# Other places in the tile for the split weights, sums taken earlier, and activations split ahead of weights, in a decoder layer

## The chip, the core and the metric

The kernel runs on one core of a Trainium2 chip. The metric is the device time of one execution in microseconds (us), the median of three runs. A separate execution was taken by the hardware profiler; everything that is said of single instructions comes from it. The engines are called as the profile calls them: PE does the matrix products (PEld is its loading of the stationary operand), DVE and ACT are the vector and the scalar engine, POOL a general engine, and SP issues most DMAs.

## The reference

One decoder layer in float32 on 256 tokens of width 2048, cut here to what the change touches:

```python
h = rms_norm(x, mix_pre_norm)
y = hybrid_mixer(h, w_in, ..., w_branch_a, w_branch_b, w_mix_out)      # mLSTM and RWKV-7 side by side
x = x + rms_norm(y, mix_post_norm)
h = rms_norm(x, xattn_pre_norm); m = rms_norm(mem, mem_norm)
x = x + rms_norm(cross_attention(h, m, xattn_wq, xattn_wkv, xattn_wo), xattn_post_norm)
h = rms_norm(x, ffn_pre_norm)
u = h @ ffn_w_up                                                      # 2048 -> 16384
uc = conv_b + sum(conv_w[j] * shift_right(u, 2 - j) for j in range(3))
x = x + rms_norm((gelu(gate) * up) @ ffn_w_down, ffn_post_norm)       # gate, up = halves of uc
```

Nearly all of the arithmetic is in the products with the large weight matrices: `w_in`, the two branch matrices, `w_mix_out`, the four of the cross-attention, `ffn_w_up` and `ffn_w_down`.

## The kernel before

**How a product is made.** Every float32 operand of a large product is split into a high and a low part in the type float32r: high is a rounded copy (ACT), low is the rest (DVE). A product is then three products on PE: high by high, high by low, low by high. In the code `wh` and `wl` are the parts of a chunk of weights, `xh` and `xl` those of the activations.

**Blocks and chunks.** The program is a list of blocks, each 512 (or 1024) output columns wide. The weights of a block come in chunks of 512 KB: 128 partitions by 1024 floats. `run()` (L433) goes through the chunks of all blocks in one order that `visits()` lays down, 648 chunks with an index `i`. In a block of kind "fm" a chunk holds two slices (`kj`) of 512 columns; the weights are PE's stationary operand, 128 by 128 at a time, and the activations, 128 by 256, the moving one. That makes 2 slices x 4 column groups x 3 products, 24 products a chunk. The fm blocks are those of `w_in` (except four), `w_br`, `w_mo`, `w_xk`, `w_xq`, `w_xo` and `w_fu`. In a block of kind "tm" the activations are stationary and the weights move: 512 columns in four blocks of `w_in` and in `w_fd`, 296 in the small block `w_sm`, and 256 at a time in `w_xv`. The up-projection `w_fu` has the 256 chunks from i = 264, `w_fd` the 128 behind them.

**The feed.** `Feed` (L338) keeps PE supplied. `dma` loads a chunk into one of four `raw` buffers, `hi` casts it to `wh` on ACT (L376), `lo` subtracts to `wl` on DVE (L397), each a few chunks ahead of the products. `staged` (L357) gives the place of a chunk's parts in their tile: the tiles are 1152 floats long, and the 1024 floats start at an offset `o` in floats. Before, `o` is 0 for tm, and for fm it is 16, except that every fourth chunk (i divisible by 4; in the up-projection by 16) starts at 24. `wh` and `wl` have four buffers each, and the offset is the same in both.

**Side work.** Everything else (the mLSTM and RWKV recurrences, the softmax, norms, convolution) is cut into pieces by generators and put between the products by `side.half()`, which is called at each chunk and between its two slices. The engines' queues run in the order in which this program is written. The side work has small products of its own on PE: transposes (vt, haT, yT, xt), products of the recurrences (gram, lv, X, U, Tn, Y, num, den, zg), and the sums of the norms (st, stb).

**The places that the change touches.** `Stat.last` (L271) makes the norm after the last cross-attention block: it folds the sum of squares so far, squares the last two column groups on ACT, sums all over partitions by three products with ones (stb; each is two instructions on PE), and takes Ln and Exp on ACT. Until that is done the up-projection's first products can't start. The last `w_xo` block is "bankwise": all its products for the first two column groups come first, then those of the third, then those of the fourth, which goes to a bank of its own (`apart`), so that the squares can begin early. In `run()` the chunks that a block holds back for such an order are the `tail`: two here, four at the end of `w_fd`. For a tail the weights' parts are made first (`feed.lo`), and then the activations' parts are asked for (`b["xs"]`), which for `w_fd` splits them at that moment (`asplit`). In the program's first block the three products of a column group follow each other, wl last.

Of the kernel before, what the change touches and what calls it, by code (L numbers as in the profile page):

```python
# [11 lines left out]
AF = mybir.ActivationFunctionType  # L12
# [133 lines left out]
def _layer(ctx, tc, nc, d, dbg):  # L146
# [21 lines left out]
    def C(name, tag, shape=None, dt=F32):  # L168
        return mp.tile(shape or [P, S], dt, tag=tag, bufs=1, name=name)
# [73 lines left out]
    class Stat:  # L243
# [24 lines left out]
        def fold(self):  # L268
            dve.tensor_add(self.acc[:, 0], self.acc[:, 0], self.acc[:, 1])

        def last(self, src, tag, meanwhile):  # L271

            self.fold()
            sq = C("sql", tag, [P, 2, S])
            for j in range(2):
                act.activation(sq[:, j], src[j], AF.Square)
            q = aux("stb", [P, S])
            for i, v in enumerate((self.acc[:, 0], sq[:, 0], sq[:, 1])):
                mm(q, ones.broadcast_to((P, P)), v, start=(i == 0), stop=(i == 2))
            meanwhile()  # L280
            self.rb = cp.tile([P, S], F32, tag="strb", bufs=1, name=self.name + "_b")
            act.activation(self.rb, q, AF.Ln, scale=1.0 / D, bias=epsc)
            act.activation(self.rb, self.rb, AF.Exp, scale=-0.5)
            self.done = True

# [38 lines left out]
    def block(kind, srcs, xs, evac, before=None, cols=512, pool_=None, pre=None, bankwise=False, tail=0):  # L324
# [2 lines left out]
                           pool=pool_ or acc, pre=pre, task=None, bankwise=bankwise, tail=tail))  # L327
        return blocks[-1]

    class Feed:  # L330
        def __init__(self, order):
            self.kind = [k for k, s in order]
# [38 lines left out]
        def hi(self, upto):  # L371
# [60 lines left out]

    def run():  # L433
        order = visits()
        feed = Feed([(b["kind"], s) for b, c0, c1 in order for s in b["srcs"][c0:c1]])
        feed.begin()
        for c in range(1, 8):
            x_load(c)
# [3 lines left out]
        for b, c0, c1 in order:  # L442
# [23 lines left out]
            for ci, s in enumerate(srcs):  # L466
                if b["pre"]:
                    b["pre"](ci, feed)
                feed.lo(i + 1)
                side.half()  # L470
                side.more = lambda: feed.hi(i + 2)
                ahead = b["xs"](k)
                feed.lo(i + 3)
                feed.dma(i + 6)
                wh, wl = feed.st.pop(i)
                for kj in range(s.shape[1]):
                    xh, xl = b["xs"](k) if kj else ahead
                    first, last = k == 0, k == nk - 1
                    if b["kind"] == "fm":
                        steps = []  # L480
                        for m in range(nm):
                            o = banks[m // 2][:, m % 2]
                            a, c = wh[:, kj, m * P:(m + 1) * P], wl[:, kj, m * P:(m + 1) * P]
                            steps.append([(o, a, xh, first and m % 2 == 0, False), (o, c, xh, False, last),
                                          (o, a, xl, False, False)])
                        if first and entry and b is entry[0]:
                            steps = [[v[0] for v in steps], [v[1] for v in steps], [v[2] for v in steps]]
                        else:
                            steps = [[v[0], v[2], v[1]] for v in steps]
# [860 lines left out]
    def y_evac(b, st, key, gname):  # L1350

        def gen(ps):
# [1 line left out]
                M[key] = [U("z0"), U("z1")]  # L1354
            z = M[key][b // 2]

            last = [ps[1][:, 0], xo3["apart"]] if b == 3 and key == "z2" else []

            def carry(g, js=(0, 1)):
                for j in js:  # L1360
                    m = (b % 2) * 4 + g * 2 + j
                    act.activation(z[:, m], last[j] if g and last else ps[g][:, j], AF.Copy, scale=pcol(gname, b * 4 + g * 2 + j))

            if last:
                st.add(ps[0])
                carry(0)
                st.last(last, "bg0", lambda: carry(1, (0,)))
                yield
                carry(1, (1,))
                yield  # L1370
                return
            for g in range(2):
                st.add(ps[g])
                carry(g)
# [1 line left out]
            if b == 3:  # L1376
                yield from st.column_of_sums()
        return gen

    def part(v, k2):  # L1380
        return v[k2 // 4][:, (k2 % 4) * 2:(k2 % 4) * 2 + 2]
# [276 lines left out]
        side.need(side.add(xo()))  # L1658

    for b in range(4):  # L1660
        xo3 = block("fm", W("w_xo", b), lambda k: (M["oT"][:, 0, k], M["oT"][:, 1, k]), y_evac(b, st3, "z2", "xpostg"),
              before=need_o if b == 0 else None, bankwise=b == 3)


    stf = Stat("stf")
# [289 lines left out]
```

## Time and profile before

| | |
|---|---|
| median of three runs | 1885.58 us (1885.05 to 1885.87) |
| the profiled execution | 1884.58 us |
| its span in the trace | 1882.5 us |
| granted clock of PE | 0.999 |
| fm products (128x256), all kinds | 11,328, mean duration 277 to 281 ns |
| tm products of 512 columns with `as` | 1,536, mean duration 389 to 390 ns |
| ACT casts to `wh` (L376) | 640, mean 1043 ns |
| DVE subtractions to `wl` (L397) | 640, mean 1217 ns |

Times in the trace count from the start of the span. Products on PE overlap: one lasts some 280 ns in the profile, but the next starts some 115 ns after it. So a product's cost is read from start to start, or as the length of a stretch through its count. The duration of a matmul is modelled at its end, and moves with that distance only in part. In a row of the timeline the first number is the start and the second the duration, both in us; what stands in brackets is the idle time ahead of the instruction and what ended it.

### The profile page before, as it was taken

Reading aid. Unit: us, or ns where it says so; the run is one execution under the profiler, and the core shown is the slowest. Engines: PE = TensorE matmul, PEld = TensorE weight load, DVE = VectorE, ACT = ScalarE, POOL = GpSimd, SP = SyncE. Lnnn points to the kernel's source line nnn. Section 1 sums busy time; section 2 is a strip of 40 time slices with the busy share of each in tenths; the row PEclk is TensorE's granted clock in tenths of the full one; section 3 lists DMA queues with packets and bytes.
Section 4 is the critical chain, followed back from the end, with each engine's and each line's share of the span. In section 5 each row is a group of like instructions: output and inputs, shape, how many; then the busy total and the mean of one; then the engine's idle time right before and its main releaser. Section 6 shows DMA issues by size and latency. Waiting matters only on the chain.

```text
span 1882.5 us, 36361 instructions
## 1 busy us (share of the span) xinstructions
PE 1872.3 (99%) x15024; PEld 1783.9 (95%) x15024; DVE 1293.9 (69%) x1832; ACT 1016.4 (54%) x1477; POOL 21.3 (1%) x40
## 2 busy tenths in 40 slices
PE   9999999999999999999999999999999999999998
PEld 9999988999999999999999999999999988888886
DVE  7788787566675857677766666677666675556555
ACT  6776445555454645666554445554454555445544
POOL 0000000000000000000000000000000000000000
PEclk9999999999999999999999999999999999999999
DMA  7545544344556765455666666666666666666664
GB/s 260 187 163 198 179 146 161 131 147 157 169 174 209 265 204 182 138 193 180 190 190 192 197 194 192 193 189 192 196 196 193 195 191 214 194 193 194 192 192 142
DMA packets 98197, 351.46 MB, mean 187 GB/s; under 512 B 11056, under 2 KB 11568, under 8 KB 97648
## 3 DMA queue, kind: packets, MB, share of 16 engines
q1 hardware_dynamic: 97168, 348.01, 57.8%
q8 instruction: 117, 1.92, 0.4%
q10 hardware_dynamic: 864, 1.15, 0.2%
q14 instruction: 48, 0.39, 0.1%
HBM read 347.01 MB, written 2.10 MB: 185 GB/s over the span
## 4 chain that ended last, share of the span: by engine, by line
PE 97%; DVE 1%; ACT 1%; DMA 0%; issue 0%; ACTq 0%; DVEq 0%
PE fm L181 68%; PE tm L181 25%; DVE wl L397 1%; PE gram L181 0%; PE Y L181 0%; PE lv L181 0%; PE num L181 0%; ACT wh L376 0%; DMA w<-in_w_in_dram 0%; DVE rows L66 0%; PE X L181 0%; PE gramA L181 0%; PE U L181 0%; PE zg L181 0%; PE zwa L181 0%
## 5 line engine op out<-in xcount | busy, mean ns | idle before, releaser
L397 DVE TENSOR_TENSOR wl<-raw,wh 128x1024 fp32r<-128x1024 f32 (+1 forms) x640 | 776.2, 1217 | 428.9 <-ACT wh L376 424.5
L376 ACT CAST wh<-raw 128x1024 fp32r<-128x1024 f32 (+1 forms) x640 | 664.8, 1043 | 512.8 <-PE fm L181 387.2
L181 PE MATMUL fm<-fh,wh 128*128 128x256 f32 x2048 | 567.3, 277 | 1.4 <-ACT fh L66 1.4
L181 PE MATMUL fm<-fh,wl 128*128 128x256 f32 x2048 | 566.5, 277 | 0.0
L181 PE MATMUL fm<-fl,wh 128*128 128x256 f32 x2048 | 566.3, 277 | 0.0
L181 PEld LDWEIGHTS fm<-fh,wh 128*128 128x128 f32 x2048 | 384.9, 188 | 1.5 <-ACT fh L66 1.5
L181 PEld LDWEIGHTS fm<-fh,wl 128*128 128x128 f32 x2048 | 384.9, 188 | 0.2 <-DVE wl L397 0.2
L181 PEld LDWEIGHTS fm<-fl,wh 128*128 128x128 f32 x2048 | 384.9, 188 | 0.0
L181 PE MATMUL tm<-wh,as 128*128 128x512 f32 x1024 | 315.8, 390 | 0.8 <-DVE as L66 0.8
L181 PE MATMUL fm<-hh,wh 128*128 128x256 f32 x1024 | 287.7, 281 | 0.0
L181 PE MATMUL fm<-hh,wl 128*128 128x256 f32 x1024 | 285.7, 279 | 1.2 <-DVE wl L397 1.0
L181 PE MATMUL fm<-hl,wh 128*128 128x256 f32 x1024 | 285.3, 279 | 0.0
L181 PEld LDWEIGHTS tm<-wh,as 128*128 128x128 f32 x1024 | 192.2, 188 | 40.9 <-DVE as L66 1.1
L181 PE MATMUL tm<-wl,as 128*128 128x512 f32 x512 | 199.3, 389 | 0.0
L181 PEld LDWEIGHTS fm<-hh,wl 128*128 128x128 f32 x1024 | 193.0, 188 | 2.1 <-DVE wl L397 1.4
L181 PEld LDWEIGHTS fm<-hh,wh 128*128 128x128 f32 x1024 | 193.4, 189 | 1.3
L181 PEld LDWEIGHTS fm<-hl,wh 128*128 128x128 f32 x1024 | 193.1, 189 | 0.1
L181 PEld LDWEIGHTS tm<-wl,as 128*128 128x128 f32 x512 | 96.1, 188 | 20.0
L66 ACT CAST as<-ac 128x256 fp32r<-128x256 f32 x128 | 45.6, 404 | 110.8 <-PE tm L181 110.8
L66 DVE TENSOR_TENSOR as<-ac,as 128x256 fp32r<-128x256 f32 x128 | 48.6, 421 | 61.7 <-ACT as L66 61.7
L181 PE MATMUL fm<-mgh,wh 128*128 128x256 f32 x256 | 71.4, 279 | 0.0
L181 PE MATMUL fm<-mgl,wh 128*128 128x256 f32 x256 | 71.2, 278 | 0.0
(383 smaller groups left out, 2223.9 us busy)
## 6 DMA issues: line engine op xcount, KB each, us to landing
raw<-in_w_fu_dram SPq DMA_DIRECT2D x256, 512.0 KB, 4.2
raw<-in_w_in_dram SPq DMA_DIRECT2D x152, 512.0 KB, 3.5
raw<-in_w_fd_dram SPq DMA_DIRECT2D x128, 512.0 KB, 3.9
raw<-in_w_br_dram SPq DMA_DIRECT2D x32, 512.0 KB, 3.8
raw<-in_w_mo_dram SPq DMA_DIRECT2D x32, 512.0 KB, 4.2
raw<-in_w_xk_dram SPq DMA_DIRECT2D x8, 512.0 KB, 3.6
raw<-in_w_xv_dram SPq DMA_DIRECT2D x8, 512.0 KB, 3.6
raw<-in_w_xq_dram SPq DMA_DIRECT2D x8, 512.0 KB, 3.8
```

Source lines behind the costliest of these rows:

```text
L66: return f(out, *a, **k)
L181: pe.matmul(out, lhsT, rhs, start=start, stop=stop, skip_group_check=True)
L376: nc.scalar.copy(wh, r)
L397: nc.vector.tensor_sub(wl, r, self.st[self.nl][0])
```

## The change

It has five parts.

1. The places. For fm chunks `o` is now 24 throughout. For tm it stays 0 where 512 columns move, and becomes 8 for the small block and for `w_xv`, which gets a kind of its own in the feed. A table `KICK` names 22 chunks, all of kind fm, that have one half at another place: with 0 the first slice lies at 16 and the second at 24, with 1 the first at 24 and the second at 48 (16 beyond a multiple of 32). They stand at the begin of a stretch behind side products, or in the middle of a chunk where these come between its slices. The regular change of place every four or sixteen chunks is gone.
2. The first block. For the first two chunks the products go by groups of four: all high by high, then activations low, then weights low.
3. The tails. The activations' parts are asked for ahead of the weights' parts.
4. The last `w_xo` block. The squares and the sum of its first two column groups, and the fold, come directly after those groups and ahead of the next weights. Ahead of the last six products the square of the third group is taken, and the products with ones for the fold and for this square are made. Only the fourth group's square and product come after the last product.
5. `Stat.last` keeps Ln and Exp; the products with ones are in `ones_of`.

```diff
-        def last(self, src, tag, meanwhile):
-
-            self.fold()
-            sq = C("sql", tag, [P, 2, S])
-            for j in range(2):
-                act.activation(sq[:, j], src[j], AF.Square)
-            q = aux("stb", [P, S])
-            for i, v in enumerate((self.acc[:, 0], sq[:, 0], sq[:, 1])):
-                mm(q, ones.broadcast_to((P, P)), v, start=(i == 0), stop=(i == 2))
-            meanwhile()
+        def ones_of(self, vs, start=False, stop=False):
+            if start:
+                self.q = aux("stb", [P, S])
+            for i, v in enumerate(vs):
+                mm(self.q, ones.broadcast_to((P, P)), v, start=start and i == 0, stop=stop and i + 1 == len(vs))
+
+        def last(self):
...
+    KICK = {16: 0, 26: 1, 32: 0, 52: 1, 60: 0, 104: 0, 108: 0, 111: 0, 116: 0, 117: 1, 120: 1, 134: 0, 140: 0, 144: 1,
+            159: 1, 168: 0, 215: 0, 218: 1, 235: 0, 242: 0, 256: 0, 280: 1}
...
             k, c = r.shape[1:]
-            up = i - len(self.src) + 384
-            o = 0
-            if self.kind[i] == "fm":
-                o = 16 if i % (16 if up >= 0 else 4) else 24
+            kick = KICK.get(i)
+            e = -(-c // 64) * 64
+            o = 24 if self.kind[i] == "fm" else 0 if c >= 512 and self.kind[i] == "tm" else 8
+            if kick is not None:
+                o, e = (16, e + 8) if kick == 0 else (o, e + 24)
             w = wp.tile([P, 1024 + 128], F32R, tag=name, bufs=4, name=name)
-            e = -(-c // 64) * 64
             return w[:, o:o + k * e].rearrange("p (k c) -> p k c", k=k)[:, :, 0:c]
...
-        feed = Feed([(b["kind"], s) for b, c0, c1 in order for s in b["srcs"][c0:c1]])
+        feed = Feed([("xv" if b is xv else b["kind"], s) for b, c0, c1 in order for s in b["srcs"][c0:c1]])
...
+                        elif b is blocks[0] and k < 4:
+                            steps = [[v[0] for v in steps], [v[2] for v in steps], [v[1] for v in steps]]
...
             if nt:
 
+                ahead = [b["xs"](k + j) for j in range(sum(s.shape[1] for s in tail))]
                 feed.lo(i + nt - 1)
...
-                        steps.append((w[0][:, kj], w[1][:, kj]) + tuple(b["xs"](k)))
+                        steps.append((w[0][:, kj], w[1][:, kj]) + tuple(ahead[len(steps)]))
...
+                            if g and ti == 2 * n - 2:
+                                b["mid"](banks)
...
                     if g == 0:
+                        if b["bankwise"]:
+                            b["after"](banks)
                         feed.lo(i + 1)
...
+    def y_last(b, st, key, gname):
+        def carry(src, m):
+            act.activation(M[key][b // 2][:, (b % 2) * 4 + m], src, AF.Copy, scale=pcol(gname, b * 4 + m))
+
+        def after(ps):
+            st.add(ps[0])
+            st.fold()
+
+        def mid(ps):
+            M["sql"] = C("sql", "bg0", [P, 2, S])
+            act.activation(M["sql"][:, 0], ps[1][:, 0], AF.Square)
+            for j in range(2):
+                carry(ps[0][:, j], j)
+            st.ones_of((st.acc[:, 0], M["sql"][:, 0]), start=True)
+
+        def gen(ps):
+            end = xo3["apart"]
+            act.activation(M["sql"][:, 1], end, AF.Square)
+            st.ones_of((M["sql"][:, 1],), stop=True)
+            carry(ps[1][:, 0], 2)
+            st.last()
+            yield
+            carry(end, 3)
+            yield
+        return after, mid, gen
```

More of the change, by code (lines that the diff above doesn't have):

```diff
@@ L269, in fold @@
             dve.tensor_add(self.acc[:, 0], self.acc[:, 0], self.acc[:, 1])
-        def last(self, src, tag, meanwhile):
-            self.fold()
-            sq = C("sql", tag, [P, 2, S])
-            for j in range(2):
-                act.activation(sq[:, j], src[j], AF.Square)
-            q = aux("stb", [P, S])
-            for i, v in enumerate((self.acc[:, 0], sq[:, 0], sq[:, 1])):
-                mm(q, ones.broadcast_to((P, P)), v, start=(i == 0), stop=(i == 2))
-            meanwhile()
+        def ones_of(self, vs, start=False, stop=False):
[4 more added lines that the diff above has]
+        def last(self):
             self.rb = cp.tile([P, S], F32, tag="strb", bufs=1, name=self.name + "_b")
-            act.activation(self.rb, q, AF.Ln, scale=1.0 / D, bias=epsc)
+            act.activation(self.rb, self.q, AF.Ln, scale=1.0 / D, bias=epsc)
             act.activation(self.rb, self.rb, AF.Exp, scale=-0.5)
@@ L1355, in gen, with carry @@
             z = M[key][b // 2]
-            last = [ps[1][:, 0], xo3["apart"]] if b == 3 and key == "z2" else []
-            def carry(g, js=(0, 1)):
+            def carry(g, js=(0, 1), src=None):
                 for j in js:
                     m = (b % 2) * 4 + g * 2 + j
[L1362 to L1371, printed above, removed]
+                    act.activation(z[:, m], ps[g][:, j] if src is None else src, AF.Copy, scale=pcol(gname, b * 4 + g * 2 + j))
             for g in range(2):
@@ L1660, in _layer @@
     for b in range(4):
-        xo3 = block("fm", W("w_xo", b), lambda k: (M["oT"][:, 0, k], M["oT"][:, 1, k]), y_evac(b, st3, "z2", "xpostg"),
-              before=need_o if b == 0 else None, bankwise=b == 3)
+        after, mid, gen = y_last(b, st3, "z2", "xpostg")
+        xo3 = block("fm", W("w_xo", b), lambda k: (M["oT"][:, 0, k], M["oT"][:, 1, k]),
+                    gen if b == 3 else y_evac(b, st3, "z2", "xpostg"), before=need_o if b == 0 else None, bankwise=b == 3)
+        xo3["after"], xo3["mid"] = after, mid
     stf = Stat("stf")
```

## The prediction

> **What bounds the kernel now.** I read the page first, for who is busy, then the chain of work that ended last, for where the rate changes, and then single rows of the timeline at the edges of weight chunks.
>
> ```profile
> PE 1872.3 (99%) x15024; PEld 1783.9 (95%) x15024; DVE 1293.9 (69%) x1832; ACT 1016.4 (54%) x1477; POOL 21.3 (1%) x40
> ...
> PE 97%; DVE 1%; ACT 1%; DMA 0%; issue 0%; ACTq 0%; DVEq 0%
> ```
>
> PE is busy for 99% of the span and is 97% of the chain; DVE and ACT, which prepare its weights, have a third and a half of their time free. So the time is the number of products times the distance from one product's start to the next. The chain shows that this distance is not one number:
>
> ```profile
> 95.88 29.45 PE fm L181 x252
> 539.75 129.86 PE fm L181 x1128
> 953.53 572.11 PE fm L181 x5028
> ```
>
> The columns are start, length and count. The same 128x256 "fm" product takes 116.9 ns (29.45 us / 252) in the first piece, 115.1 in the second, 113.8 in the third. No piece has a wait in it. What differs is the place of the weights in their tile, which `staged` sets by the chunk's index: in the early part every fourth chunk starts at float 24 and the others at 16; in the up-projection one in sixteen starts at 24. The second piece holds 47 chunks, 12 of them at 24; the third 209.5, of them 13. With f for a product at 16 and f + d at 24: f + 0.255 d = 115.12 and f + 0.062 d = 113.78, so d is 6.9 ns and f 113.35. The timeline confirms it at the edges of chunks (24 products each). The first three rows begin chunks 176 (at 24), 177 and 178 (at 16):
>
> ```profile
> 561.63 0.28 PE L181 MATMUL fm<-hh,wh 128*128 128x256 f32 x1
> ...
> 564.52 0.28 PE L181 MATMUL fm<-hh,wh 128*128 128x256 f32 x1
> ...
> 567.25 0.28 PE L181 MATMUL fm<-hh,wh 128*128 128x256 f32 x1
> ```
>
> At 24: 2.88 us (120.2 ns a product). At 16, right behind it: 2.73 us (113.5). Place is not all, though. The next rows are chunk 159, whose second half follows eight transposes, and the begins of 160 (at 24), 161 (at 16) and 164:
>
> ```profile
> 511.18 1.04 PE L1170 MATMUL yT<-con,ysb 128*128 128x128 f32 x8
> 512.18 0.28 PE L181 MATMUL fm<-hl,wh 128*128 128x256 f32 x1
> ...
> 513.48 0.28 PE L181 MATMUL fm<-hh,wh 128*128 128x256 f32 x1
> ...
> 516.29 0.28 PE L181 MATMUL fm<-hh,wh 128*128 128x256 f32 x1
> ...
> 524.77 0.28 PE L181 MATMUL fm<-hh,wh 128*128 128x256 f32 x1
> ```
>
> Behind the transposes, products at 16 are 118.2 ns apart (1.30 us / 11); chunk 160 at 24 has 117.1; the three chunks at 16 behind it 117.8 (8.48 / 72). So a rate outlives its cause. I call the four cases A (place 16, 113.4), B (16, 117.8), C (24, coming out of A, 120.2) and D (24, out of B, 117.1).
>
> **The main part: the places.** The change makes 24 the place of every fm chunk and keeps 16 for one half of 22 chunks (`KICK`), each at or behind certain side products. So what counts is the rate of products that stay at 24. In the trace of before I find 120 or 117 at 24 and nothing below. Two patterns of the new kernel can be read directly. A kick of kind 1 is: side products, 12 products at 16, then 24. Chunk 159 was just that, with 16 left in B, and 24 then ran at 117.1. Chunk 147, with the U products in its middle, is the same with 16 left in A; then chunk 148 at 24 begins and ends here:
>
> ```profile
> 477.00 0.28 PE L181 MATMUL fm<-ha,wh 128*128 128x256 f32 x1
> ...
> 479.88 0.28 PE L181 MATMUL fm<-ha,wh 128*128 128x256 f32 x1
> ```
>
> That is 120.0. And 24 directly behind side products, with no stay at 16 (chunk 108, behind the den and num products; from its second product to the next chunk, 23 products):
>
> ```profile
> 335.70 0.28 PE L181 MATMUL fm<-hl,wh 128*128 128x256 f32 x1
> ...
> 338.40 0.28 PE L181 MATMUL fm<-hh,wh 128*128 128x256 f32 x1
> ```
>
> 117.4. So I expect a kernel at 24 to move between D and C. The up-projection has its last side products near its start and no kick behind them: D, which costs 117.25 - 113.35 = 3.9 ns a product. Its 32 blocks of 8 chunks of 24 products, less one kicked half, are 6132 products: 23.9 us. The other fm chunks are 216 by the code's blocks (128 of w_in, 32 each of w_br and w_mo, 8 each of w_xk, w_xq and w_xo), 5184 products, 252 of them in kicked halves: 4932 at 24. D costs 19.2 us there, C 6.8 ns a product or 33.5; a kick that lands in A hands over C, one that lands in B hands over D. About two thirds D gives 24.0. The 264 products in kicked halves cost between 0 (A) and 4.4 ns (B): 0.6 us. Sum after: 48.5 us above 113.35.
>
> What goes away: in the up-projection 16 chunks x 24 x 6.9 ns = 2.6 us; in the early part 5184 products at between 1.8 ns (the clean piece of 539.75) and 3.5 (the piece of 95.88) over f, 9.3 to 18; most of it looks like the clean piece, so I take 11. Together 13.6. The places cost 48.5 - 13.6 = +35 us.
>
> On the cause a page speaks against any effect of place. The Trainium skill (SBUF — State Buffer, "Who interferes with whom") gives TensorE two independent read ports, one for weights and one for the moving operand, and says that it never waits on anyone. The rows above disagree: the same product, with nothing to wait for, costs 120.2 or 113.5 ns by the weights' offset. By that page this part would be worth 0.
>
> **xv and the small block.** Their moving weights go from place 0 to 8:
>
> ```profile
> 740.88 5.76 PE tm L181 x48
> ```
>
> xv products are 120.0 ns apart now, as in C; 192 of them at best gain 6.7 ns each (1.3 us), at worst stay or lose a little. The 96 products of the small block have 296 columns, and in proportion can gain or lose half as much per product and column: 0.7 us either way. No row shows place 8; relative to the other operand it is 32 bytes off a 64-byte step as 24 is, so I take 0, with -2.0 to +0.7.
>
> **The start.** For chunks 0 and 1 the weights' low part is now used last, in blocks of four.
>
> ```profile
> 9.49 0.28 PE L181 MATMUL fm<-hl,wh 128*128 128x256 f32 x1
> 10.45 0.38 PE L181 MATMUL fm<-hh,wl 128*128 128x256 f32 x1 [0.68 <-DVE wl L397]
> ```
>
> Of chunk 1, two products ran before the wait for wl that ends at 10.45. Eight can run there now (0.9 us of the 1.0 up to 10.45), so six products, 0.68 us, move under the wait. DVE and ACT keep their order. I take -0.7; if the first chunk waits elsewhere, 0.
>
> **Entry sums.** In the last xo block two of the three sums of squares move ahead of the last six products.
>
> ```profile
> 817.16 0.28 PE L181 MATMUL fm<-oT,wl 128*128 128x256 f32 x1
> 817.30 0.67 PE L181 MATMUL stb<-st,ones 128*128 128x256 f32 x2
> 817.48 0.38 ACT L66 ACTIVATE sql<-fm 128x256 f32<-128x256 f32 x1 [0.97 <-PE fm L181]
> ...
> 817.81 1.03 PE L181 MATMUL stb<-sql,ones 128*128 128x256 f32 x4
> ...
> 818.87 0.47 ACT L66 ACTIVATE st_b<-stb,mhalf 128x256 f32<-128x256 f32 x1 [0.65 <-PE stb L181]
> ```
>
> Today PE runs all six stb products (1.37 us) without a gap while ACT takes the last square under them. Afterwards four of the six, about 0.9 us, stand in front of the last fm products and push them back by as much; then PE stands idle for the last square and does the last two. The logarithm starts 1.71 us behind the last oT product's start today (818.87 - 817.16); from the same point it will be 0.9 + 0.32 (to the square's start, 817.48 - 817.16) + 0.38 + 0.67 = 2.27. So ACT's logarithm comes some 0.6 us later, not earlier. The added wait, of the early sums for the fold on DVE and the first square on ACT, has the six fm products and everything after them queued behind it; both are ready by then, as the fold no longer stands behind a wl split of 1.23 us. I take +0.6 (0 to +0.9); a gain is excluded, since the last square can't come sooner and two products still follow it.
>
> **The tail.** The last activations are split ahead of the last weights.
>
> ```profile
> 1862.76 1.05 ACT L376 CAST wh<-raw 128x1024 fp32r<-128x1024 f32 x1 [1.67 <-PE tm L181]
> 1863.71 0.71 ACT L66 CAST as<-ac 128x256 fp32r<-128x256 f32 x2
> 1863.84 1.23 DVE L397 TENSOR_TENSOR wl<-raw,wh 128x1024 fp32r<-128x1024 f32 x1 [1.50 <-ACT wh L376]
> ...
> PE tm L181 <- DVE as L66: 0.8, 1, 0.8
> ```
>
> PE waits 0.8 us for `as`, which stands behind wh on ACT and wl on DVE. Put first, the splits fit into the idle 1.67 us of ACT and 1.50 us of DVE that stand ahead of wh and wl, and need no buffer that PE still holds. Next late is the last wl, at 1865.07, which the sixth product behind needs about then. I take -1.0 (-0.8 to -1.2).
>
> **Sum.** +35 + 0 - 0.7 + 0.6 - 1.0 = +34. The profiled execution took 1884.58 us (span 1882.5); 1918.6 for it, and the median of the runs stands 1.0 above it: 1919.6.
>
> **Rivals.**
> Forecast, 24 is C or D throughout, chance 0.52. D everywhere costs 23.9 + 19.2 - 13.6 = 29.5 us, and with the small terms at their good ends (-3.9) it is +26: 1911. C in half of the up-projection as well (3066 x 2.9 ns = 8.9 us) gives +43: 1929; C everywhere 41.7 + 33.5 - 13.6, or +62: 1947. Its own range is 1911 to 1938.
>
> A rate of 113.4 that belongs to 24, chance 0.40. The rate is not set by place alone: 16 has two rates, 24 has two, and a step through 24 has turned B into A. If the case is a phase between weight loads and products that is shifted by changes of place, then 24 may run as well as 16 once it is in phase, the kicks put it right after each disturbance, and before's trace never stays at 24 longer than one chunk to show it. Point from which it decides: products inside a chunk at 24 come 113.4 apart. Then 13.6 us go, 264 kicked products cost up to 6.8 ns (1.8 us), xv gives half a us to one, the small terms -1.1: about -13.6, 1872 (1868 to 1876). Against it: every chunk at 24 that I read, out of A, out of B and behind side products, was above 117 ns from its first products to its last.
>
> The place has no price of its own, chance 0.04: C and D are what a change of place costs, and fade when the place stays; but B fades as little. If that held for half of the products, gain and loss cancel and only the start, the sums and the tail are left, -1.1, 1884.5. That the weights' place has no price at all is what the page named above implies; the rows of chunks 176 and 177 all but exclude it. The remaining 0.04 is a mixture in which about a third of the products have 113.4.
>
> **How the numbers follow.** 0.2% is 3.8 us, about what a measurement of this kernel tells from no change. Faster by more: 0.42 (the second case and part of the mixture). Within: 0.06. Slower: 0.52. Cases of both signs hold most of the chance, so the range must hold both: 1868 to 1932; left out are the upper end of the forecast's own range and a little below.
>
> **What would show it.** Right: in the piece of the up-projection without side products the chain has 117 to 120 ns per product, and the mean of an fm matmul rises from 277 ns to 280 or more. Wrong: 113.4 there. The start: no wait for wl at 10.45 longer than 0.3 us. The sums: the first st_b activation more than 1.71 us behind the last oT product's start, with a gap of PE between the two groups of stb. The tail: no wait of PE for `as`.

## The result and the profile after

The changed kernel takes 1927.2 us in the median (1926.7 to 1927.7) against 1885.5 for the kernel before: 2.2% slower, ratio 1.0221 (95% interval 1.0204 to 1.0239). The forecast was 1919.6. The profiled execution took 1927.1 us, with a span of 1925.0 (before 1882.5), so the trace has 42.5 us more to account for.

From the page of the changed kernel, busy time by engine and one of the six big groups of products (busy time, mean ns of one, idle time ahead of them):

```profile
PE 1916.0 (100%) x15024; PEld 1828.4 (95%) x15024; DVE 1296.7 (67%) x1832; ACT 1018.9 (53%) x1477; POOL 21.0 (1%) x40
...
L181 PE MATMUL fm<-fh,wh 128*128 128x256 f32 x2048 | 575.6, 281 | 1.4 <-ACT fh L66 1.4
```

The same group in the kernel before:

```profile
L181 PE MATMUL fm<-fh,wh 128*128 128x256 f32 x2048 | 567.3, 277 | 1.4 <-ACT fh L66 1.4
```

Hardly any idle time is new: PE is busier by 43.7 us with the same 15,024 instructions. The products themselves have become dearer. The chain of work that ended last says where; the first three pieces answer to those of before (29.45, 129.86 and 572.11 us):

```profile
95.97 29.77 PE fm L181 x252
...
545.16 135.31 PE fm L181 x1128
...
971.23 598.09 PE fm L181 x5040
```

The piece of 252 products has hardly changed, 116.9 to 118.1 ns each. The second has gone from 115.1 to 120.0, the up-projection from 113.8 to 118.7. The last is a rate that the prediction doesn't know. It stands in the timeline of the changed kernel as the distance between the begins of chunks 400 and 408, 192 products:

```profile
1227.39 0.28 PE L181 MATMUL fm<-fh,wh 128*128 128x256 f32 x1
...
1250.18 0.28 PE L181 MATMUL fm<-fh,wh 128*128 128x256 f32 x1
```

22.79 us / 192 = 118.7 ns. I call it E, beside A to D. It is there almost from the start: chunks 264 and 265 still run at 117.3, and from chunk 267 to chunk 279 (their begins) it is E already:

```profile
844.16 0.28 PE L181 MATMUL fm<-fh,wh 128*128 128x256 f32 x1
...
878.34 0.28 PE L181 MATMUL fm<-fh,wh 128*128 128x256 f32 x1
```

34.18 us / 288 = 118.7 ns. Early chunks have it too: 43 to 58, 145 to 149, 160 to 163 and 219 to 234.

Averaged over all products with neither wait nor side product behind them, the early fm blocks went from 115.5 to 118.5 ns and the up-projection from 113.8 to 118.7. Above 113.35 that is 26.2 us now against 10.9 in the early blocks, and 32.5 against 2.9 in the up-projection: together +44.9 us.

**The small parts.** The moving weights of xv at place 8 (740.88 and 5.76 us before):

```profile
753.42 5.61 PE tm L181 x48
```

116.9 ns instead of 120.0, and 0.5 us over all 192. At the start, chunk 0 begins at 5.19 us (5.17 before), and chunk 2 here:

```profile
12.59 0.28 PE L181 MATMUL fm<-hh,wh 128*128 128x256 f32 x1
```

Before, it began at 13.06, so 0.47 us are won, but chunk 16 begins at 43.48 against 43.51: the chunks between, now at 24, have eaten the gain. The waits of PE in the changed kernel (total, times, longest):

```profile
PE fm L181 <- ACT fh L66: 1.4, 1, 1.4
...
PE stb L181 <- ACT sql L66: 0.5, 1, 0.5
PE fm L181 <- ACT wh L387: 0.3, 1, 0.3
```

The waits for `as` (0.8) and for the first `wl` (0.7) are gone and one of stb for `sql` has come. The timeline around the entry sums shows its place:

```profile
830.11 0.64 PE L181 MATMUL stb<-st,ones 128*128 128x256 f32 x2
...
830.59 0.59 PE L181 MATMUL stb<-sql,ones 128*128 128x256 f32 x2
...
831.62 0.28 PE L181 MATMUL fm<-oT,wl 128*128 128x256 f32 x1
831.93 0.38 ACT L66 ACTIVATE sql<-fm 128x256 f32<-128x256 f32 x1 [1.23 <-PE fm L181]
...
832.37 0.70 PE L181 MATMUL stb<-sql,ones 128*128 128x256 f32 x2 [0.47 <-ACT sql L66]
...
833.11 0.47 ACT L66 ACTIVATE st_b<-stb,mhalf 128x256 f32<-128x256 f32 x1 [0.42 <-PE stb L181]
```

Four stb instructions stand ahead of the last products and push them back; then PE waits 0.47 us for the last square and does the other two. From the first product of the last xo chunk to the first of the up-projection it is 7.59 us, 6.75 before: +0.84, of which 24 products at 24 are 0.16. At the end of the program, DVE and ACT now have the activations done ahead of the last weights:

```profile
1905.96 0.75 DVE L66 TENSOR_TENSOR as<-ac,as 128x256 fp32r<-128x256 f32 x2
1906.45 1.06 ACT L376 CAST wh<-raw 128x1024 fp32r<-128x1024 f32 x1 [1.05 <-PE tm L181]
```

The chunk in which PE waited for `as` takes 2.73 us instead of 3.94: -1.2. In sum: places +44.9, xv -0.5, small block +0.1, tail -1.2; what is left of the 42.5, -0.8, is the entry sums (+0.8), the start (-0.5) and the steps from a product to the next across side products, which are 1.1 us shorter in sum.

### The profile page after: what moved, and what is told of

Read it like the earlier page. It is cut to its first block, busy times and chain, and to the rows that moved or that the text cites. A ratio compares the mean times of both kernels' runs of the same rounds, so it can differ in the third digit from the quotient of the medians.

```text
span 1925.0 us, 36356 instructions
## 1 busy us (share of the span) xinstructions
PE 1916.0 (100%) x15024; PEld 1828.4 (95%) x15024; DVE 1296.7 (67%) x1832; ACT 1018.9 (53%) x1477; POOL 21.0 (1%) x40
## 4 chain that ended last, share of the span: by engine, by line
PE 99%; ACT 0%; DMA 0%; DVE 0%; issue 0%; ACTq 0%
PE fm L181 70%; PE tm L181 25%; PE gram L181 0%; PE Y L181 0%; PE lv L181 0%; PE num L181 0%; DMA w<-in_w_in_dram 0%; PE X L181 0%; PE gramA L181 0%; PE U L181 0%; PE zg L181 0%; PE zwa L181 0%; PE xsc L181 0%; PE xt L1804 0%; PE xo L181 0%; PE stb L181 0%
## 5 line engine op out<-in xcount | busy, mean ns | idle before, releaser
L181 PE MATMUL fm<-fh,wh 128*128 128x256 f32 x2048 | 575.6, 281 | 1.4 <-ACT fh L66 1.4
L181 PE MATMUL fm<-fh,wl 128*128 128x256 f32 x2048 | 574.7, 281 | 0.0
L181 PE MATMUL fm<-fl,wh 128*128 128x256 f32 x2048 | 574.6, 281 | 0.0
L181 PE MATMUL fm<-mgh,wl 128*128 128x256 f32 x256 | 72.1, 282 | 0.0
```

Of the source, the lines that this page charges most:

```text
L181: pe.matmul(out, lhsT, rhs, start=start, stop=stop, skip_group_check=True)
```

## The experiments

The theory: the rate of a product is set by the place of its weights, 24 has no rate of 113.4, and side products and changes of place only choose among the rates that a place has. Against it stood that kicks or other edits cost the time, and that the rate is a phase that any place can have.

**1. The places exchanged.**

```diff
-            o = 24 if self.kind[i] == "fm" else 0 if c >= 512 and self.kind[i] == "tm" else 8
+            o = 16 if self.kind[i] == "fm" else 0 if c >= 512 and self.kind[i] == "tm" else 8
...
-                o, e = (16, e + 8) if kick == 0 else (o, e + 24)
+                o, e = (24, e + 24) if kick == 0 else (o, e + 8)
```

> All edits of the changed kernel, but 16 and 24 exchanged: fm chunks at 16, and the 22 kicked halves at 24. Theory (the rate belongs to the place of the weights, and 24 has no rate of 113.4 ns): the 26.2 + 32.5 us that the changed kernel spends above 113.35 ns a product go, except 1.8 us in kicked halves and some stretches at 117.8, so 1871 to 1877 us. First rival (what costs is being kicked, whichever place is the base): about as long as the changed kernel, over 1915. Second rival (the cost is in the other edits): over 1900 as well.

1878.2 us (1876.3 to 1878.8): 49 us less than the changed kernel, and 0.4% below the kernel before, ratio 0.9956 (0.9941 to 0.9971). Just above the expected span. The chain:

```profile
537.94 127.96 PE fm L181 x1128
...
949.81 571.22 PE fm L181 x5040
```

113.4 and 113.3 ns a product in the two pieces that had 120.0 and 118.7. The other edits and the kicked chunks are the same; only the two places are exchanged. Both rivals fall.

**2. The other edits without the places.** All else is as in the changed kernel.

```diff
-            kick = KICK.get(i)
...
-            o = 24 if self.kind[i] == "fm" else 0 if c >= 512 and self.kind[i] == "tm" else 8
-            if kick is not None:
-                o, e = (16, e + 8) if kick == 0 else (o, e + 24)
+            up = i - len(self.src) + 384
+            o = 0
+            if self.kind[i] == "fm":
+                o = 16 if i % (16 if up >= 0 else 4) else 24
```

> All edits of the changed kernel except the places, which are those of the kernel before (16 with a periodic 24, xv and the small block at 0). Theory (the loss is the places): start -0.5, entry sums +0.7, tail -1.2, so 1884 to 1885 us, about 1 us below the kernel before. Rival (the moved sums and splits delay work elsewhere): several us above the kernel before.

1885.3 us (1883.9 to 1886.8), the kernel before 1886.2 beside it: ratio 0.9995 (0.9986 to 1.0005). No difference that can be measured, and none near the rival's. The trace has the terms: tail -1.21, the stretch with the entry sums 7.58 against 6.75 us. The profiled execution also waited for its first loads longer than that of before, which hides the start:

```profile
PE fm L181 <- ACT wh L387: 1.6, 1, 1.6
```

**3. 16 throughout, no kicks.**

```diff
-            kick = KICK.get(i)
+            kick = None
...
-            o = 24 if self.kind[i] == "fm" else 0 if c >= 512 and self.kind[i] == "tm" else 8
+            o = 16 if self.kind[i] == "fm" else 0 if c >= 512 and self.kind[i] == "tm" else 8
```

> Fm chunks at 16 everywhere, no chunk at 24, the other edits as in the changed kernel. Theory (side products leave 16 at 117.8 ns and only a step through 24 brings it back to 113.4): long stretches at 117.8; if all fm products run so, 11316 x 4.45 = 50 us above the best, 1920; if the up-projection is at 113.4, 1893. Rival (side products leave nothing behind at a constant place): 113.4 throughout, about 1870.

1876.6 us in a single run, within the range of the kernel with 22 kicks (1876.3 to 1878.8). The early blocks average 114.3 ns, the up-projection 113.6. The theory's own picture was too gloomy: side products do leave B behind (chunks 60 to 65, 108 to 113, 159 to 163 and 235 to 239 run at 117.8, and 242 to 249 behind products of xv), but other side products put A back without any change of place (zg at 164, stb at 218 and 281). Chunks 266 to 280 run at 117.8 as well, and no side product stands at that change: it comes in chunk 266, where the first load of a `wl` slice waits 0.15 us for DVE. The kernel before had the same wait there and stayed at 113.3, so a short wait seems able to change the rate, but need not. The rival's "nothing is left behind" is wrong too. What the kicks of experiment 1 bring is no more than they cost: the early blocks had 114.6 there.

**4. A sweep of places.**

```diff
+            if 264 <= i < 520:
+                o = (0, 4, 8, 12, 16, 20, 24, 28, 32, 40, 48, 56, 64, 72, 80, 88,
+                     24, 0, 48, 8, 64, 16, 40, 24, 56, 12, 80, 16, 28, 20, 32, 4)[(i - 264) // 8]
```

> Only the up-projection differs from the changed kernel: its 256 chunks go through 16 places, 8 chunks (192 products) at each, first in rising order (0, 4, 8, 12, 16, 20, 24, 28, 32, 40, 48, 56, 64, 72, 80, 88 floats) and then in another. Theory (the place sets the rate): a place has nearly the same rate both times; 16 and 48 (and 80) run at 113.4 or 117.8, 24 at 117 to 120, and 0, 8, 32, 40 and 56 are above 113.4 too. Rival (only a change of place costs and the rate is a phase): the two visits of a place differ as much as two places do, and rates of 113.4 are met at many places.

In the timeline, the begins of stretches of 192 products in the second order of places: 0, 48, up to the begin of 8; then 16, 40, 24, up to the begin of 56; then 80, 16, up to the begin of 28:

```profile
1228.65 0.28 PE L181 MATMUL fm<-fh,wh 128*128 128x256 f32 x1
...
1251.69 0.28 PE L181 MATMUL fm<-fh,wh 128*128 128x256 f32 x1
...
1273.45 0.28 PE L181 MATMUL fm<-fh,wh 128*128 128x256 f32 x1
...
1319.21 0.28 PE L181 MATMUL fm<-fh,wh 128*128 128x256 f32 x1
...
1341.82 0.28 PE L181 MATMUL fm<-fh,wh 128*128 128x256 f32 x1
...
1364.85 0.28 PE L181 MATMUL fm<-fh,wh 128*128 128x256 f32 x1
...
1387.38 0.28 PE L181 MATMUL fm<-fh,wh 128*128 128x256 f32 x1
...
1432.39 0.28 PE L181 MATMUL fm<-fh,wh 128*128 128x256 f32 x1
...
1454.16 0.28 PE L181 MATMUL fm<-fh,wh 128*128 128x256 f32 x1
...
1475.92 0.28 PE L181 MATMUL fm<-fh,wh 128*128 128x256 f32 x1
```

0 takes 23.04 us (120.0 ns a product), 48 behind it 21.76 (113.3). 16, out of 64, takes 22.61 (117.8), 40 23.03 (119.9), 24 22.53 (117.3). 80, out of 12, takes 21.77 and 16 behind it 21.76, 113.3 each. By the means of the chunks: 16, 48 and 80 ran at 113.3 to 113.5 in four of their seven visits and at 117.8 in the other three. No other place came below 116.6 in any of its visits: 0 and 64 had 120.0, 4 and 8 118.3, 20 118.8, 28 and 40 120.0, 32 118.6, 72 118.3; 24 (three visits) and 88 (one) had 117.3; 12 and 56 changed between visits. So among these places 113.4 is had only at 64 bytes beyond a multiple of 128 (16, 48, 80 floats), and 24 hasn't got it. The theory holds, with more rates to a place than one.

**5. The sweep with moved activations.** The tiles `fh` and `fl` are 32 floats longer and their data begins at 16.

```diff
-        return mp.tile([P, KD, S], F32R, tag="hT", bufs=2, name=name)
+        t = mp.tile([P, KD * S + 32], F32R, tag="hT", bufs=2, name=name)
+        o = 16 if name in ("fh", "fl") else 0
+        return t[:, o:o + KD * S].rearrange("p (k s) -> p k s", k=KD)
```

> The sweep over 16 places again, with the activations of the up-projection (fh, fl) moved by 16 floats; nothing else differs from the first sweep. Theory 1 (what counts is the place of the weights alone): again 113.4 ns only at 16, 48 and 80 floats, and 117 to 120 at 0, 32 and 64. Theory 2 (what counts is the distance of the weights' place from the activations'): 113.4 at 0, 32 and 64, and 117 to 120 at 16, 48 and 80.

Neither: no place had 113.4; all lay between 116.6 and 120.0. What the expectation overlooked is that the longer tile moves the second buffer too: the low part lies 16,512 bytes behind the high one here, and not 16,384. (These distances are worked out from the code, with the two buffers taken to lie side by side; the trace shows no addresses.)

**6. A table of kicks.** In the up-projection, groups of eight chunks: one at 40, three at 48, one (first half or whole) at p, three at 16.

```diff
+            if 264 <= i < 520:
+                t, m = divmod(i - 264, 8)
+                p = (0, 4, 8, 12, 20, 24, 28, 32, 36, 40, 44, 52, 56, 60, 64, 72)[t % 16]
+                if m == 0:
+                    o = 40
+                elif m < 4:
+                    o = 48
+                elif m == 4:
+                    o, e = (p, e if t >= 16 else e + (16 - p) % 32)
+                else:
+                    o = 16
```

> Only the up-projection differs from the changed kernel: 32 groups of 8 chunks: one at 40 floats, three at 48 (which came out at 117.8 ns behind 40 in the sweep), one kicked to another place p, three at 16. The p are 0, 4, 8, 12, 20, 24, 28, 32, 36, 40, 44, 52, 56, 60, 64 and 72; in the first 16 groups only the first half of the chunk is at p, in the others all of it. Theory (a rate is a phase that a change of place hands over): for a given p the last three chunks are all at 113.4 or all at 117.8, the same for half and whole chunks, and 12 gives 113.4. Rival (the change of place always restores the good phase): 113.4 behind every p. Other rival (chance): half and whole chunks differ.

48 behind 40 came out at 113.4 this time, in all groups but the first, from whichever rate the chunk at 40 was entered; 117.8 in the first sweep was no property of 40. So all kicks but the first start from A. Whole chunks at 0 (from 1205.17), then 16 (from 1208.05, three chunks up to 1216.53); and at 12 (1271.96), then 16 (1274.78 to 1282.95):

```profile
1205.17 0.28 PE L181 MATMUL fm<-fh,wh 128*128 128x256 f32 x1
...
1208.05 0.28 PE L181 MATMUL fm<-fh,wh 128*128 128x256 f32 x1
...
1216.53 0.28 PE L181 MATMUL fm<-fh,wh 128*128 128x256 f32 x1
...
1271.96 0.28 PE L181 MATMUL fm<-fh,wh 128*128 128x256 f32 x1
...
1274.78 0.28 PE L181 MATMUL fm<-fh,wh 128*128 128x256 f32 x1
...
1282.95 0.28 PE L181 MATMUL fm<-fh,wh 128*128 128x256 f32 x1
```

8.48 us / 72 = 117.8 behind 0, 8.17 / 72 = 113.5 behind 12: place and side work are the same, only the step before differs. Behind 0 and 64 it was B with halves and wholes (the half at 0 was entered from B), behind 8, 12, 20, 24, 28, 40, 52, 56, 60 and 72 it was A with both; 4, 32, 36 and 44 gave one with the half and the other with the whole. So a step hands a rate over, a repeatable one for 12 of 16 places, and neither "the same for half and whole" nor "always restored" holds.

**7. 16 without kicks, the entry sums of before.** Made from the kernel before: 16 for fm, xv and the small block, the start and the tail of the change.

```diff
-            up = i - len(self.src) + 384
-            o = 0
-            if self.kind[i] == "fm":
-                o = 16 if i % (16 if up >= 0 else 4) else 24
+            o = 0 if c >= 512 and self.kind[i] == "tm" else 16
```

> 16 for all fm chunks without kicks, 16 for xv and the small block as well, the start and the tail of the change, the entry sums as in the kernel before. Against the run with 16 and no kicks (1876.6): theory (the moved sums cost 0.7 us) gives -0.7 for the sums, and between 0 (117 ns as at 8) and -0.7 (113.4) for xv: 1875.2 to 1876. Rival (the moved sums gain, as they stand ahead of the last product): 1877 or more.

1876.6 us (1876.2 to 1878.4), ratio to the kernel before 0.9958 (0.9941 to 0.9975): between what the theory and the rival gave, and no difference from experiment 3 that can be told. In the trace the stretch from the last xo chunk to the up-projection is 6.75 us against 7.57 at the same place 16, so the moved sums cost 0.8; but xv came out at 117.8 and the early blocks at 114.8, since other chunks fell into B. The small term is real and is lost among the rates.

**8. Steps through 40.** Experiment 7 with 12 whole chunks at 40.

```diff
+            if i in (26, 53, 61, 67, 112, 135, 160, 216, 236, 243, 257, 266):
+                o = 40
```

> The run with the old sums and 16 for all fm chunks (1876.6), with 12 whole chunks at 40 floats (26, 53, 61, 67, 112, 135, 160, 216, 236, 243, 257, 266), each at or near the start of a stretch that ran at 117.8 there. Theory (a step through 40 ends in the good rate of 16, as in 13 of 13 visits out of 16 or 48 in the run with kicked groups): about 41 chunks go from 117.8 to 113.4, 41 x 24 x 4.45 ns = 4.4 us, less 1.2 us in the 12 chunks at 40: 1873.4. Rival (what the kicks do is chance): no gain, 1876 to 1878.

1876.1 us (1874.8 to 1876.5), ratio to the kernel before 0.9946 (0.9932 to 0.9959): the lowest median of all runs, but not clearly below experiment 7; by the time alone, the rival stands. Nine of the 12 steps ended in 113.4; those at 26, 61 and 216 ended in 117.8. In the trace, everything behind the first two chunks is 2.6 us shorter than in experiment 7, where the theory had 3.2 (4.4 less 1.2). These rows, the waits for the first loads in experiment 8 and then in 7, show what took 1.2 of it in the profiled execution:

```profile
PE fm L181 <- ACT wh L386: 2.0, 1, 2.0
```

```profile
PE fm L181 <- ACT wh L384: 0.8, 1, 0.8
```

**9. The changed kernel with steps through 40 in the up-projection.**

```diff
+            if i in (267, 283, 299):
+                o = 40
```

> The changed kernel with three whole chunks of the up-projection (267, 283, 299) at 40 instead of 24. Theory (118.7 ns in the changed kernel's up-projection is a third phase of 24, and behind 40 it comes out at 117.3, as in the sweep): about 240 chunks x 24 x 1.4 ns = 8 us less than the changed kernel, 1919. Rival (118.7 is what a long stay at 24 costs): the time of the changed kernel, 1927.

1927.5 us; the time of the changed kernel. But not for the rival's reason. Behind 267 the up-projection ran at 117.3 for 12 chunks, behind 283 at 118.7, behind 299 at 117.3 again, until the xt transposes at 302 put it into 118.7, where it stayed:

```profile
971.63 598.09 PE fm L181 x5040
```

The step did give D, twice of three times; the last side product has the last word, and I had set the step ahead of it. E isn't what a long stay costs: chunks 268 to 279 kept 117.3 here, and in the changed kernel E came in the third chunk. It is a state that something leaves behind, and the xt transposes are one such thing, not the only one. In the changed kernel E begins in chunk 266, ahead of the first xt and in a chunk without side products, where the first product with that chunk's `wl` comes 0.03 us late; a wait for this `wl` is likely, since it was ready only 0.05 us before its load, but no row shows one. In the early blocks E begins behind ssk (42) and behind the kicked halves that follow X and lv (144), yT (159) and stb (218). (In experiment 12 below, where the place changes from block to block, a block at 24 goes from 117.3 to 118.7 at the transposes of 298, and the later blocks at 24 are at 117.3.)

**10. Activations moved by 32 floats.** Against experiment 5:

```diff
-        o = 16 if name in ("fh", "fl") else 0
+        o = 32 if name in ("fh", "fl") else 0
```

> The sweep over 16 places with the activations of the up-projection moved by 32 floats (128 bytes) instead of 16. Theory (what counts is the place of both operands within 128 bytes): as in the first sweep, 113.4 ns is met at 16, 48 and 80 floats alone. Rival (moving the activations at all, or the longer tiles, takes the good rate away): no 113.4 anywhere, as with 16.

No 113.4 again. The same stretch as in experiment 4, from the begin of 48 to that of 8:

```profile
1251.29 0.28 PE L183 MATMUL fm<-fh,wh 128*128 128x256 f32 x1
...
1273.90 0.28 PE L183 MATMUL fm<-fh,wh 128*128 128x256 f32 x1
```

22.61 us, 117.8 ns, against 21.76. So a place within 128 bytes isn't enough, and the theory in that form falls. A clue stands in a stretch that wasn't meant to change, the four tm blocks of `w_in`, whose stationary operand is the activations. The changed kernel, and experiment 10:

```profile
253.14 43.74 PE tm L181 x192
```

```profile
254.95 44.57 PE tm L183 x192
```

227.8 and 232.1 ns. Here `hh` hasn't moved; `hl` has, by the 128 bytes of the longer tile. That suggests the distance between the two parts.

**11 and 12. The distance between the parts.** Slices of `fh` and `fl` are moved by quarters of a block, in tiles 32 and 128 floats longer, while the weights' place goes through 16, 0, 24, 8, 48, 40 from block to block.

```diff
+            o = sk[1] * S + self.at[sk[1] // 4]
+            return self.t[:, o:o + S]
...
+        t = mp.tile([P, KD * S + 32], F32R, tag="hT", bufs=2, name=name)
+        if name in ("fh", "fl"):
+            return Slices(t, ((0, 16, 32, 32), (0, 0, 0, 16))[name == "fl"])
...
+            if 280 <= i < 520:
+                o = (16, 0, 24, 8, 48, 40)[(i - 280) // 8 % 6]
```

In 12 the tile is `KD * S + 128` long and the moves are (0, 64, 128, 128) and (0, 0, 0, 64).

> Only the up-projection is read. The weights' place goes by block through 16, 0, 24, 8, 48, 40 floats. The tiles of the activations are 32 floats (128 bytes) longer, so the low part lies 16,512 bytes behind the high one instead of 16,384, and each quarter of a block moves its slices: high and low by (0, 0), (16, 0), (32, 0) and (32, 16) floats. Theory 1 (what counts is the distance between the two parts of the activations, the same within 128 bytes not being enough): 113.4 ns at places 16 and 48 in the third quarter alone, where the distance is 16,384 again. Theory 2 (the longer tile or a moved high part takes the good rate away): no 113.4 in any quarter. Theory 3 (the low part's own place counts): none in the quarters 1 to 3, which share it.

> As the run before, with tiles 128 floats (512 bytes) longer and quarters moved by (0, 0), (64, 0), (128, 0) and (128, 64) floats, that is distances of 512, 256, 0 and 256 bytes beyond 16,384. Theory 1 (the distance between the parts counts): 113.4 at 16 and 48 in the third quarter, and in the others only if their distances are whole periods: in the first with a period of 512 bytes, in all with one of 256. Theory 2 (a moved high part or a longer tile): none.

Experiment 11, a block at 48: the begins of its quarters, of the second chunk of the third, and its end. The third quarter is the one in which the low part lies 16,384 bytes behind the high one:

```profile
1113.80 0.28 PE L192 MATMUL fm<-fh,wh 128*128 128x256 f32 x1
...
1119.42 0.28 PE L192 MATMUL fm<-fh,wh 128*128 128x256 f32 x1
...
1125.22 0.28 PE L192 MATMUL fm<-fh,wh 128*128 128x256 f32 x1
...
1127.96 0.28 PE L192 MATMUL fm<-fh,wh 128*128 128x256 f32 x1
...
1130.68 0.28 PE L192 MATMUL fm<-fh,wh 128*128 128x256 f32 x1
...
1136.40 0.28 PE L192 MATMUL fm<-fh,wh 128*128 128x256 f32 x1
```

117.1, 120.8, then 114.2 and 113.3, and 119.2 ns. The good rate is back in the third quarter alone, in the same program, with the same weights. The blocks at 16 had 117.5 to 117.9 in that quarter (B). Experiment 12, a block at 16, the begins of its quarters and its end (that of the block at 0 behind it):

```profile
1021.20 0.28 PE L192 MATMUL fm<-fh,wh 128*128 128x256 f32 x1
...
1026.64 0.28 PE L192 MATMUL fm<-fh,wh 128*128 128x256 f32 x1
...
1032.08 0.28 PE L192 MATMUL fm<-fh,wh 128*128 128x256 f32 x1
...
1037.52 0.28 PE L192 MATMUL fm<-fh,wh 128*128 128x256 f32 x1
...
1042.96 0.28 PE L192 MATMUL fm<-fh,wh 128*128 128x256 f32 x1
```

5.44 us / 48 = 113.3 in each quarter, at distances of 16,384 plus 512, 256, 0 and 256 bytes. 48 was in B, 117.8, in all its blocks. 0, 24, 8 and 40 kept the rates of the first sweep, 120.0, 117.3, 118.3 and 120.0, but for the block at 24 named under 9, and the tm blocks of `w_in` were at 43.74 us again. So the longer tile did no harm, nor did a high part moved by 256 or 512 bytes. In all runs the good rate came under two conditions only: the parts of the activations a multiple of 256 bytes apart (tried: 0, 64, 128, 256 and 512 bytes beyond 16,384), and the weights 64 bytes beyond a multiple of 128. Theory 1 of both runs holds, with a period of 256 bytes; which of 16 and 48 is in A and which in B it didn't foresee.

Not tried, and open: whether the weights' 64 bytes count from the activations' place or from the start of memory (activations moved by 16 floats at a kept distance would tell), what in the chip makes the places matter, and by what rule side products and short waits choose among the rates of a place.

## Why the prediction was right, and where a size was off

**The range.** The sign was forecast with a chance of 0.52 against 0.42, and the range, 1868 to 1932, held outcomes of both signs; that the time lies in it says little. The central value, +34 us, was 8.5 too low against the profiled execution (+42.5). What counts is the mechanism, term by term.

**What bounds the kernel.** Right: products by their distance, no wait. PE's busy time grew by 43.7 us, the span by 42.5.

**24 has no rate of 113.4.** Right, and shown: no chunk at 24 averaged below 117.1 in any kernel with the parts of the activations at their old distance, nor below 116.7 in the others. The step from reading three patterns of the old trace to a whole kernel at 24 held. The rival with a chance of 0.40, that 24 is as good as 16 once in phase, named its point of decision: products inside a chunk at 24 that come 113.4 apart. The sweep visited 24 three times, 192 products each: 117.3 each time. The third rival, no price of place, falls by the same table. The Trainium skill (SBUF — State Buffer, "Who interferes with whom") gives TensorE two independent read ports, from which no price of place would follow; the runs disagree, with 113.3 against 120.0 ns for the same product by place alone.

**The up-projection in D.** This is the term that was mis-sized. The prediction put the up-projection at 117.25 ns, 23.9 us; it ran at 118.7, 32.5 us. I read two rates at 24, and there are three. The reason that I gave, last side products near the start and then no more, was the right place to look, but I took the rate behind den and num for the rate behind any side product; the xt transposes can leave another (experiment 9), and in the changed kernel it had set in at chunk 266, ahead of them and with no side product beside it. That is 8.6 us of error, against a miss of 8.5 between the profiled executions (7.6 between the medians); the other errors, 1.6 in the early blocks and small ones of the other sign, about cancel.

**The early blocks.** Forecast 24.0 and 0.6 for the kicks, measured 26.2 with both. The share of two thirds D was a guess, and it came out well by luck: 65 of the 216 chunks ran in C, most of them in the piece of 1128 products at 120.0, and the others in D or E. E is what the sum lacked: 41 chunks x 24 x 1.35 ns = 1.3 us. The rule for the kicks held exactly where the kicked half is at 16: of the 14 kicks of kind 0, the eight that ran at 113.4 there came out at 120.0, the six at 117.8 came out at 117.3. It didn't hold for kind 1. I read that kind from chunk 159 of the kernel before, where the half is at 16, but in a kick of kind 1 it is at 48. The one kick that ran at 113.4 there (26) handed over D, and of those at 117.8, 117 and 120 handed over D, but 52, 144, 159 and 218 E.

**What goes away.** Forecast 13.6, measured 13.8.

**xv** came out between its bounds, on the good side, -0.5. **The start** won 0.47 of the 0.7 forecast up to chunk 2. **The entry sums:** forecast +0.6, measured 0.84 less 0.16 for the place in that chunk, and 0.8 in the pair of runs at 16. The test that I named for it, the logarithm over 1.71 us behind the last oT product, was badly chosen: it is 1.49 (833.11 - 831.62), since four stb instructions stand ahead of that product now. The wait of PE between the two groups of stb is there as forecast, 0.47. **The tail:** -1.2 against -1.0.

## What to carry to other kernels

Products with no wait in sight can still have several rates; read them from start to start over whole stretches, and compare stretches that differ in one address. Before choosing the place of an operand, sweep it in one run, and keep the other operands' distances fixed while doing so: padding a tile moves its neighbours. Where a rate is a state that side work leaves behind, ask which side product comes last before the longest stretch, since its rate is paid there.

## What the runs showed of the hardware that was not expected

- One 128x256 product in float32r took from 113.3 to 123.3 ns (place 12 in the sweep) by the places of its operands and the state that earlier work had left, at a granted clock of 0.999.
- 113.3 was had only with the weights at 64 bytes beyond a multiple of 128 and the two parts of the activations a multiple of 256 bytes apart. At place 48 of experiment 11, 128 bytes more between them cost 4 ns a product (117.1), 64 bytes more 6 to 7 (119.2 and 120.8). Where the activations were stationary and 512 columns moved, 128 bytes more cost 4 ns (227.8 to 232.1).
- With the parts 16,384 bytes apart, products at 16, 48 and 80 floats had two lasting rates, 113.3 and 117.8, at 24 three, 117.3, 118.7 and 120.0. E lasted for 210 chunks where no side product stood (the piece of 5040 products of the changed kernel). Eight transposes changed a rate (113.3 to 117.8 in the middle of chunk 159 of the kernel before), and so, it seems, did a wait of 0.15 us (chunk 266 in experiment 3).
